# Values of memory heads 1 to 3 turned by VectorE and DMAs, and read nine steps later

## Chip, cores, metric

The kernel runs on one core of a Trainium2 chip. The time is the device time of one execution in microseconds (us); lower is better. The engines are TensorE (PE in the profile; PEld are its weight loads), VectorE (DVE), ScalarE (ACT), GpSimd (POOL) and SyncE (SP), whose queue issues nearly all DMAs here.

## What is computed

One inference step of a layer with two branches: a matrix memory (mLSTM, 4 heads of 512) and an HGRN2 branch (8 heads of 128), merged by sigmoid gates. There are 512 prompt frames and 32 sample frames, 544 columns in all, and the model's width is 1024. Of the reference, the part around the change:

```python
proj = xn @ w_in[l]
u, v_m, z_m, ... = jnp.split(proj, ...)           # v_m: the memory's values, 4 heads x 512
c = silu(causal_conv(u));  qm = c @ w_qm;  km = c @ w_km * M_HD ** -0.5     # per head
s = jnp.einsum('bhtd,bhsd->bhts', q, k) * dmat
num = w_inter[..., None] * jnp.einsum('bhed,bhtd->bhte', C, q) + jnp.einsum('bhts,bhse->bhte', s, v)
h = num / jnp.maximum(jnp.abs(den), jnp.exp(-m_t))[..., None]
C_new = decay[..., None, None] * C + jnp.einsum('bhs,bhse,bhsd->bhed', w_last, v, k)
hm = (head_layernorm(h) + m_skip[l] * c) * jax.nn.silu(z_m)
ya = hm @ w_brm[l]
```

Both products that use v sum over frames, so v is needed with frames on the partitions. The projection leaves it the other way, with channels on the partitions.

## The kernel before

Products are made in fp32r: each operand is split into a high part (ScalarE's copy) and a low part (VectorE's difference, L205 for weights), and three matmuls replace one (high x high, high x low, low x high). Memory heads go one after another; each has its keys (k), queries (q), scores (sc, L1054), then `mchain`, then the branch product `stage_br` (ya, L229), which adds to a sum kept in DRAM.

Between these pieces TensorE works through a list of input projections, the *pump*. A projection unit for the heads is a *pair* (class `Two`) of two channel tiles, made by a seven-product scheme in blocks a11, s2, a12, s3, s1, a22, s4; consecutive pairs overlap. A block is two *steps*, a step is six matmuls of 272 columns (line L575, tile d). For heads 1 and 2 the list is values v0/v1, v2/v3, gates z0/z1, z2/z3, and the next head's conv inputs u0/u1, u2/u3: 84 steps. For head 3 it is v, z and the first HGRN unit: 70 steps. By the order in which the blocks are sorted, v1, v0, v3, v2 are finished after steps 14, 18, 28 and 32, z1, z0, z3, z2 after 42, 46, 56 and 60, u1 and u0 after 70 and 74. `pump.when` holds these numbers, `pump.done` counts steps made.

`mchain` is a generator. A `yield n` in it lets TensorE do n more steps before what follows is put into its order; TensorE's order is thus written out by hand, and what is ready early has no influence on it. All other engines and SP's queue are ordered by the scheduler at build time, each queue then runs in order. After the last v (step 32), before the change:

- four blocks b of 128 frames, each after the gap that VTGAP gives: four transposes of v on TensorE into a PSUM buffer (tile vt, L1210; two such buffers rotate), ScalarE's high part vh (L1213), VectorE's low part vl (L1214);
- the sample's 32 frames: POOL makes three copies side by side (vsm, L963), four transposes (vts, L1222), the split into vs;
- four steps, then the old memory's split (c0p, c0h, c0l) where it isn't done yet and the numerators: matmuls nm (L1313, the sample's L1289), with the new sample memory Cs (L1241) between them. Cs takes one of the four PSUM buffers with tag "h", which the pairs use as well: two to a pair, the first from its first block on, the second from its a12;
- VectorE's normalisation; for heads 1 and 2 the weighed keys are read back from DRAM (kwl, L1155), and six and three steps later the prompt's new memory is made (C, L1112); eleven steps after that y is turned back in four groups a step apart (yt, L1366), with hm made from each (L1372 to L1374, L147) as input of `stage_br`. In head 3, whose new memory comes at the kernel's end, yt comes fourteen steps after the numerators or when its z is done. Then the pump runs out and `stage_br` starts.

In heads 1 and 2 the numerators start at step 41 and the first yt stands at step 61; in head 3 they start at 42.

The keys of heads 1 to 3 are already turned another way, by `turn` (L973 to 979): VectorE transposes each 32 by 32 block in place (L975), and four DMAs write the tile to DRAM so that blocks land transposed, in runs of 32 floats; a later DMA reads frames as rows.

## Time and profile before

| | |
|---|---|
| median of 3 runs | 1104.61 us (1103.64 to 1105.09) |
| profiled execution | 1106.07 us, span in the trace 1104.3 us |
| TensorE busy | 1089.9 us (99%) |
| VectorE busy | 920.8 us (83%) |
| ScalarE busy | 712.2 us (64%) |
| GpSimd busy | 173.0 us (16%) |
| DMA queue of SP | 40.0% of 16 engines' time, 137.10 MB |

Busy times are sums over the span of 1104.3 us. Matmuls overlap in TensorE's array and their ends are modelled, so intervals between starts tell more than durations. In rows of the timeline the columns are start, duration, engine, line, operation, and out<-in by the program's names; a bracket gives the engine's idle time before the row and what ended it.

### The profile page before, as it was taken

The numbers are of one execution on the slowest core, as the hardware profiler recorded it, in microseconds if no ns is written. First come the engines' busy times: TensorE is split into PE (matmuls) and PEld (weight loads), VectorE is DVE, ScalarE is ACT, GpSimd is POOL, SyncE is SP. The second block draws the span as 40 slices with busy tenths as digits, with TensorE's granted clock in tenths as the row PEclk, the third lists the DMA queues.
The fourth block names the chain that finished last, engine by engine and source line by source line (L and its number), as shares of the span: only waits on it lengthen the run. The fifth ranks groups of instructions, "written<-read, shape, count | busy, mean of one in ns | idle before, by whom it ended". The sixth has DMA issues, their size and how long they took to land.

```text
span 1104.3 us, 23737 instructions
## 1 busy us (share of the span) xinstructions
PE 1089.9 (99%) x8765; PEld 1077.4 (98%) x8765; DVE 920.8 (83%) x1989; ACT 712.2 (64%) x1571; POOL 173.0 (16%) x417
## 2 busy tenths in 40 slices
PE   9999999999999999999999999999999999999998
PEld 9999999999999999999999999999999999999998
DVE  6986999679798596986898688999999888789885
ACT  6686656755666455664566478887777767445762
POOL 2122024111010130101100123322332100000000
PEclk9999999999999999999999999999999999999999
DMA  6223225634365344464556222122221353343743
GB/s 224 78 96 107 83 86 174 146 100 127 105 206 160 81 147 144 126 225 92 157 159 218 95 78 84 56 80 80 85 75 62 111 178 116 116 124 116 260 146 121
DMA packets 104781, 138.67 MB, mean 126 GB/s; under 512 B 35765, under 2 KB 43573, under 8 KB 104665
## 3 DMA queue, kind: packets, MB, share of 16 engines
q1 hardware_dynamic: 104496, 137.10, 40.0%
q8 instruction: 69, 1.13, 0.4%
q14 instruction: 48, 0.39, 0.1%
q10 hardware_dynamic: 168, 0.06, 0.0%
HBM read 110.96 MB, written 26.16 MB: 124 GB/s over the span
## 4 chain that ended last, share of the span: by engine, by line
PE 59%; DVE 12%; ACT 7%; issue 2%; DMA 0%; POOL 0%; DVEq 0%; ACTq 0%; POOLq 0%
PE d L575 26%; PE ya L229 6%; PE pg L2099 4%; PE yb L229 4%; PE C L1112 3%; PE q L229 3%; DVE ws L533 2%; PE k L229 2%; PE sc L1054 2%; DVE hkq L1836 2%; PE nm L1313 2%; PE ple L229 1%; DVE at L1852 1%; DVE ws L508 1%; ACT shared L1947 1%
## 5 line engine op out<-in xcount | busy, mean ns | idle before, releaser
L592 ACT COPY t<-d 128x272 f32<-128x272 f32 x126 | 47.5, 377 | 20.8 <-PE d L575 20.7
L1770 ACT COPY kmos<-hkq 128x256 f32<-128x256 f32 x56 | 23.9, 427 | 38.0 <-DVE hkq L1836 34.7
L1836 DVE TENSOR_TENSOR hkq<-hkq,hq 128x288 f32<-128x288 f32 (+1 forms) x96 | 41.4, 438 | 1.5
L1815 PE MATMUL pl<-hkq,kmos 128*128 128x128 f32 x224 | 35.5, 279 | 3.3 <-DVE hkq L1653 1.9
L801 DVE SCALAR_TENSOR_TENSOR cv<-ub,vec,cv 128x547 f32<-128x547 f32 x48 | 37.1, 782 | 0.4
L1815 PEld LDWEIGHTS pl<-hkq,kmos 128*128 128x128 f32 x224 | 30.0, 188 | 4.9 <-ACT kmos L1770 1.5
L1112 PE MATMUL C<-vh,kwl 128*128 128x256 f32 x96 | 27.0, 281 | 0.0
L1112 PE MATMUL C<-vl,kwh 128*128 128x256 f32 x96 | 26.9, 280 | 0.0
L1112 PE MATMUL C<-vh,kwh 128*128 128x256 f32 x96 | 26.8, 279 | 0.0
L1392 DVE TENSOR_TENSOR y<-ya,y 128x272 f32<-128x272 f32 x48 | 18.8, 434 | 8.0 <-PE ya L229 7.8
L1852 DVE COPY_PREDICATED at<-lmask,pl 128x256 f32<-128x256 uint8 x56 | 25.0, 446 | 0.0
L1313 PE MATMUL nm<-vh,sh 128*128 128x256 f32 x80 | 22.8, 285 | 1.0 <-ACT Co L1124 0.6
L1324 ACT COPY y<-nm 128x516 f32<-128x516 f32 x16 | 9.4, 588 | 21.5 <-PE nm L1313 21.5
L1313 PE MATMUL nm<-vl,sh 128*128 128x256 f32 x80 | 22.6, 282 | 0.0
L963 POOL COPY vsm<-vt 128x96 f32<-128x96 f32 x16 | 12.8, 809 | 62.2 <-DVE vt L599 43.9
L1313 PE MATMUL nm<-vh,sl 128*128 128x256 f32 x80 | 22.5, 281 | 0.0
L1068 ACT CAST sh<-dm 128x512 fp32r<-128x512 f32 (+3 forms) x16 | 7.4, 459 | 22.8 <-DVE dm L1062 22.8
L1054 PE MATMUL sc<-q,kh 128*128 128x512 f32 (+3 forms) x80 | 18.6, 321 | 0.0
L1243 DVE SCALAR_TENSOR_TENSOR c<-c,wi,Cs 128x256 f32<-128x256 f32 (+1 forms) x32 | 14.9, 471 | 4.1 <-PE Cs L1241 4.0
L1112 PEld LDWEIGHTS C<-vh,kwh 128*128 128x128 f32 x96 | 18.1, 189 | 0.0
L1112 PEld LDWEIGHTS C<-vl,kwh 128*128 128x128 f32 x96 | 18.1, 188 | 0.0
L1112 PEld LDWEIGHTS C<-vh,kwl 128*128 128x128 f32 x96 | 18.0, 188 | 0.0
(5767 smaller groups left out, 5164.6 us busy)
## 6 DMA issues: line engine op xcount, KB each, us to landing
ya_d<-y SPq DMA_DIRECT2D x32, 272.0 KB, 3.1
y<-ya_d SPq DMA_DIRECT2D x24, 272.0 KB, 3.1
c<-in_C SPq DMA_DIRECT2D x16, 258.0 KB, 3.6
out_Cs<-c SPq DMA_DIRECT2D x16, 258.0 KB, 2.6
out_Cp<-Co SPq DMA_DIRECT2D x15, 258.0 KB, 2.5
k_d<-kf SPq DMA_DIRECT2D x48, 68.0 KB, 2.0
x<-in_xT SPq DMA_DIRECT2D x8, 272.5 KB, 4.6
ya<-ya_d SPq DMA_DIRECT2D x8, 272.0 KB, 4.7
```

The source lines that it names most:

```text
L229: PE.matmul(both[b][:m, :TH], part(w, off + k * step, m, x), xx[:, half(b)], start=(k == 0 and j == 0), stop=(k == n - 1 and j == 2),)
L575: PE.matmul(ps, ww[:, c], xx, start=(start and k == 0 and j == 0), stop=end, skip_group_check=not start,)
L592: S.copy(t, ps)
L801: last = V.scalar_tensor_tensor(cv[:, :547], ub[:, j : j + 547], vcol(V_CW + 4 * ft + j), cv[:, :547], ALU.mult, ALU.add)
L1054: PE.matmul(pn[:, 0, :n], ks[f][x][:, j * P : (j + 1) * P], qs[f][y][:, NS + j * P : T], start=(f == 0 and i == 0), stop=(f == KH - 1 and ...
L1112: PE.matmul(pn[g], kw[b][x][:, f * P : (f + 1) * P], vv[b][y][:, VS[g]], start=(b == 0 and j == 0), stop=(b == NB - 1 and j == 2),)
L1313: PE.matmul(pn[:, g, VP[g] : VP[g] + VN[g]], st[j][x][:, (i - j) * P : (i - j + 1) * P], vv[j][y][:, VS[g]], start=(j == 0 and q == 0), st ...
L1770: S.copy(km.rearrange("p (n j c) -> p n j c", j=2, c=c), view(kk, HB, ((2 * c, NA // (2 * c)), (c - HB, 2), (1, c))),)
L1815: PE.matmul(pn[:, b * P : (b + 1) * P].rearrange("p (n j c) -> p j n c", j=2, c=c), km[:, b * P : (b + 1) * P], view(qq, b * P, ((HB + c, ...
L1836: V.tensor_tensor(x, x, t, ALU.mult)
L1852: V.copy_predicated(blocks2(at[:, :NA]), twice(lmask[:, li, :P]), blocks2(pn[:, :NA]))
L2099: PE.matmul(ps, part(w, k * P, P, x), xx[:, c], start=(k == 0 and j == 0), stop=(k == KD - 1 and j == 2))
```

## The change

For heads 1 to 3 the four transposes per block of frames and those for the sample leave TensorE. When a value tile is projected, `turn` now transposes it on VectorE in blocks of 32 by 32 and writes it to DRAM with four DMAs (16 a head). Five steps after the last value (VREAD[0]) `mchain` issues seven reads: four blocks of 128 frames into the place of vl, and the sample's frames three times. Five steps later (VREAD[1]) the splits into vh and vl start, a step apart, from SBUF and not from PSUM; four steps after the sample's split the numerators follow as before. They start at step 50 in heads 1 to 3. The first yt moves from step 61 to 70 in heads 1 and 2; in head 3 the four groups stand at steps 64 to 67 of 70. Head 0 keeps its transposes.

```diff
--- before.py
+++ after.py
@@ -40,10 +40,10 @@
 STEPS = (5, 4, 3, 4, 4, 4, 4)
 START = 2
 PDGAP = 1
-VGAPS = (0, 0, 0, 0)
+VREAD = (5, 5)
 ZN = 3
 FIRSTK, KTGAP, KWGAP = (3, 2, 1, 1, 1), (6, 14), (6, 3, 11)
-VTGAP = ((2, 1, 1, 1, 1), (1, 1, 1, 1, 1), (1, 1, 1, 1, 1), (0, 2, 2, 1, 1))
+VTGAP = (2, 1, 1, 1, 1), (0, 1, 1, 1, 1), (0, 1, 1, 1, 1), (0, 1, 1, 1, 1)
 GAPS = (20, 20, 20, 14)
 APART = 10
 FDELAY = (2, 2, 5)
@@ -820,11 +820,13 @@
         t["cc"].append(c)
         t["cs"].append(split(c[:, :T], f"cs{ft}"))
 
+    vt_d = [dr.tile([T, HD], F32, name=f"vt_d{h}") for h in range(MH)]
+
     def fill(h):
 
 
         def value(f, t):
-            st8[h]["vt"][f] = t
+            turn(vt_d[h], f, t)
 
         def gate(f, t):
             act = S.activation(t[:, :T], t[:, :T], AF.Silu)
@@ -848,7 +850,6 @@
         st8[h]["z"] = [None] * KH
         todo = []
         if h:
-            st8[h]["vt"] = [None] * KH
             todo += [pair("v", f, 16 + h * KH + f, lambda f: plain(eslot(f"vt{h}{f}")), value) for f in (0, 2)]
             todo += [pair("z", f, 32 + h * KH + f, lambda f: plain(eslot(f"z{h}{f}")), gate) for f in (0, 2)]
         else:
@@ -1199,34 +1200,46 @@
             return ch, cl
 
 
+        vv, vraw = [], []
+
+        def pair_v(b):
+            vv.append([slot(f"v{n}{h}{b}", F32R)[:, VA : VA + VW] for n in "hl"])
+            for x, y in zip(vv[b], (one4, zero4)):
+                G.tensor_copy(x[:, HD:VW], y)
+
+        def parted_v(raw, hi, dst, at=slice(None)):
+            with tc.high_priority():
+                S.copy(hi, raw)
+                return V.tensor_tensor(dst, raw[at], hi[at].bitcast(F32), ALU.subtract)
+
         if h:
-            yield max(0, max(pump.when["v", f] for f in range(KH)) - pump.done + VGAPS[h])
-        vt = t["vt"]
-        vv = []
+            yield max(0, max(pump.when["v", f] for f in range(KH)) - pump.done + VREAD[0])
+            for b in range(NB):
+                pair_v(b)
+                vraw.append(vv[b][1][:, :HD].bitcast(F32))
+                nc.sync.dma_start(vraw[b], vt_d[h][NS + b * P : NS + (b + 1) * P, :])
+            vr = slot(f"vr{h}")[: 3 * NS, :HD]
+            for i in range(3):
+                nc.sync.dma_start(vr[i * NS : (i + 1) * NS], vt_d[h][:NS, :])
+            yield VREAD[1]
         for b in range(NB):
             yield VTGAP[h][b]
-            pt = paux(f"vt{h}{b}")
+            if h == 0:
+                pair_v(b)
+                vraw.append(paux(f"vt{h}{b}")[:, 0, :])
+                for f in range(KH):
+                    PE.transpose(vraw[b][:, f * P : (f + 1) * P], t["vt"][f][:, NS + b * P : NS + (b + 1) * P], ident)
+            parted_v(vraw[b], vv[b][0][:, :HD], vv[b][1][:, :HD])
+        yield VTGAP[h][NB]
+        if h == 0:
+            vr = paux(f"vts{h}")[: 3 * NS, 0, :]
+            vsm, _ = triple(t["vt"], "vsm", t["copied"])
             for f in range(KH):
-                PE.transpose(pt[:, 0, f * P : (f + 1) * P], vt[f][:, NS + b * P : NS + (b + 1) * P], ident)
-            vh, vl = (slot(f"v{n}{h}{b}", F32R)[:, VA : VA + VW] for n in "hl")
-            with tc.high_priority():
-                S.copy(vh[:, :HD], pt[:, 0, :])
-                V.tensor_tensor(vl[:, :HD], pt[:, 0, :], vh[:, :HD].bitcast(F32), ALU.subtract)
-            G.tensor_copy(vh[:, HD:VW], one4)
-            G.tensor_copy(vl[:, HD:VW], zero4)
-            vv.append((vh, vl))
-        yield VTGAP[h][NB]
-        pt = paux(f"vts{h}")
-        vsm, copied = triple(vt, "vsm", t["copied"])
-        for f in range(KH):
-            PE.transpose(pt[: 3 * NS, 0, f * P : (f + 1) * P], vsm[:, f], ident)
+                PE.transpose(vr[:, f * P : (f + 1) * P], vsm[:, f], ident)
         vs = small("vs", [3 * NS, VW], F32R, bufs=1)
-        with tc.high_priority():
-            S.copy(vs[:, :HD], pt[: 3 * NS, 0, :])
+        lo = slice(NS, 2 * NS)
+        low = parted_v(vr, vs[:, :HD], vs[lo, :HD], lo)
         G.tensor_copy(vs[:, HD:VW], vone)
-        lo = slice(NS, 2 * NS)
-        with tc.high_priority():
-            low = V.tensor_tensor(vs[lo, :HD], pt[lo, 0, :], vs[lo, :HD].bitcast(F32), ALU.subtract)
         if h == 0:
             with tc.issue_after(low.ins):
                 for k in THEN:
```

## The prediction

> **What bounds the kernel now.** I read the page first: the span and the busy shares.

> ```profile
> span 1104.3 us, 23737 instructions
> PE 1089.9 (99%) x8765; PEld 1077.4 (98%) x8765; DVE 920.8 (83%) x1989; ACT 712.2 (64%) x1571; POOL 173.0 (16%) x417
> ```

> TensorE is busy 99% of the span, VectorE is second with 83%. So work taken from TensorE is time gained, as long as nothing makes TensorE wait. The profiled execution took 1106.07 us around its span of 1104.3; the runs' median is 1104.61, 0.13% less. I work out a difference and take it from the median. About 0.2% (2.2 us) is what a measurement of this kernel can tell from no change.

> Next I read TensorE's order where values are turned: the tile's row (min/median/max ns), then head 1's rows of the timeline, then two of the chain of waits (start, us, what).

> ```profile
> L1210 PE MATMUL vt<-ident,vt x64: 270/272/330, 111.6 to 551.4; 128*128 128x128 f32 x64
> 252.93 0.60 PE L1210 MATMUL vt<-ident,vt 128*128 128x128 f32 x4
> 254.12 0.60 PE L1210 MATMUL vt<-ident,vt 128*128 128x128 f32 x4
> 255.31 0.60 PE L1210 MATMUL vt<-ident,vt 128*128 128x128 f32 x4
> 256.94 0.66 PE L1210 MATMUL vt<-ident,vt 128*128 128x128 f32 x4 [0.29 <-DVE vl L1214]
> 258.19 0.60 PE L1222 MATMUL vts<-ident,vsm 128*96 128x128 f32 x4
> ...
> 257.60 0.75 PE d L575 x6
> 258.35 0.43 PE vts L1222 x4
> ```

> Matmuls overlap, so starts count, not durations: from one group of four transposes to the next with a step between them (six matmuls, 0.75) are 254.12 - 252.93 = 1.19 us. A group thus costs 1.19 - 0.75 = 0.44; the group for the sample's values costs 0.43. The next row shows that groups also wait: 256.94 - 255.31 = 1.63, that is 0.44 lost, because two PSUM buffers rotate and VectorE had not read the older.

> **The change, part by part.**

> 1. *Transposes out of TensorE.* Heads 1 to 3 lose four groups L1210 and one L1222 each: 15 x 0.44 = 6.6 us. All of it lies on TensorE's path.

> 2. *Waits that go with them.* TensorE's waits over heads 1 to 3 (200 to 620 us):

> ```profile
> PE Cs L1241 <- DVE c L1243: 0.9, 2, 0.6
> PE vt L1210 <- DVE vl L1214: 0.7, 2, 0.4
> PE vt L1210 <- DVE vt L599: 0.6, 1, 0.6
> ```

> The vt rows name 1.3; starts give more (0.44 where the row says 0.29), so I take 1.6. The Cs row needs counting in steps. A projection pair holds two of the four "h" PSUM buffers, the second only from its a12 block on. Numerators start at step 41 in heads 1 and 2: the pair z0/z1 still holds both (its a22 is half done), z2/z3 one, one is left, and each new-memory matmul waits until VectorE read the one before it. At step 50 z0/z1 is done, z2/z3 holds two and u0/u1 has not begun: two are left, and as in head 3, where no such row stands, they alternate. With the small losses around them 1.5 us go; zero would go if the buffers were freed late. Gains: 6.6 + 1.6 + 1.5 = 9.7.

> 3. *What VectorE and the DMAs get.* The nearest rows are those of the keys, which take this way already: instructions (min/median/max ns), DMAs (KB, us to landing), windows (length, then busy us of PE, PEld, DVE, ACT, POOL, clock, DMA share, GB/s), timeline.

> ```profile
> L975 DVE STREAM_TRANSPOSE kf<-kf x12: 731/740/746, 203.3 to 503.7; 128x544 f32<-128x544 f32 x12
> L979 SPq DMA_DIRECT2D k_d<-kf x48: 303/504/1302, 204.1 to 506.0; - x48
> k_d<-kf SPq DMA_DIRECT2D x48, 68.0 KB, 2.0
> L1155 SPq DMA_DIRECT2D kwl<-k_d x8: 382/382/391, 271.8 to 419.9; - x8
> kwl<-k_d SPq DMA_DIRECT2D x8, 256.0 KB, 5.1
> L1214 DVE TENSOR_TENSOR vl<-vt,vh x16: 681/684/692, 113.3 to 552.4; 128x512 fp32r<-128x512 f32 x16
> 240.00:248.00 8.00, 8.00 (x67) 8.00 (x67) 7.13 (x13) 5.29 (x12) 0.66 (x1) 1.00 0.82 261
> 248.00:256.00 8.00, 8.00 (x69) 8.00 (x68) 7.86 (x15) 5.57 (x12) 4.78 (x9) 1.00 0.41 135
> 249.48 0.68 DVE L205 TENSOR_TENSOR wa1236l<-wi36r,wa1236h 128x512 fp32r<-128x512 f32 x1
> 252.44 0.28 PE L575 MATMUL d<-xh,wa1236l 128*128 128x272 f32 x1
> ```

> VectorE: 12 x 0.74 = 8.9 us more, 3.0 in each head between steps 14 and 32, where (windows) it is busy 7.13 and 7.86 of 8. The cover is the lead of the weights' low parts over TensorE: 252.44 - (249.48 + 0.68) = 2.3 us at the tightest in head 1. Two transposes fall into each of the two bursts, 1.5 us against 2.3. Bounds: 0 if the lead swallows all, 8.9 if none. Nearer to the lead's end: 1.0 us in all.

> ScalarE's and VectorE's splits stay, reading SBUF for PSUM: nothing. POOL loses 12 copies for the sample (L963) and waits for nobody here: nothing.

> SP's queue: per head 16 writes at 0.50 = 8 us, 7 reads at 0.4 = 3 us. Each pair of values puts 4 us of issuing ahead of weight loads behind it, within the same lead; the DMA engines (0.82, 0.41 busy) have room. Counted in the 1.0.

> 4. *The new way's length.* Last value at step 32, numerators at 50: 18 steps x 0.75 = 13.5 us, with no TensorE transposes between. Needed: evacuation and transpose about 1.5 (two operations of 0.74 at most), four writes issued 2.0, landing 2.0, four reads issued 1.6, landing 5.1: 12.2. The first split (ScalarE's vh and VectorE's vl, 0.68 each at most) ends at 13.6, just in time. The 5.1 is for four reads in flight together, so the first may land earlier; the sample's values follow behind them, and the first new-memory matmul that reads them comes two groups of numerators later. I take 0 lost; bounds 0 and 3 a head.

> [...]

> 5. *Nine steps later: what comes next.* Numerators, the Cs stores (4 x 258 KB), key reads, C matmuls and Cp stores of heads 1 and 2 move by nine steps (6.7 us), in head 3 by eight; on SP they pass weight loads for blocks that TensorE reaches only after the C matmuls; that VectorE idles there (288 to 296 us below) says that those are ahead: 0. The last part, turning y back (yt) and making hm for the branch matmuls (ya), is now close to its reader.

> ```profile
> 304.23 14.87 PE d L575 x120
> 319.10 23.69 PE ya L229 x192
> 299.70 0.44 PE yt L1366 x4
> 300.14 0.11 PE yt L1367
> 309.68 0.68 DVE L205 TENSOR_TENSOR wa1210l<-wi10r,wa1210h 128x512 fp32r<-128x512 f32 x1
> 310.88 0.71 DVE L147 TENSOR_TENSOR hm7l<-c,hm7h 128x544 fp32r<-128x544 f32 x1
> 317.32 0.69 DVE L205 TENSOR_TENSOR wbm100l<-wbm10r,wbm100h 128x512 fp32r<-128x512 f32 x1
> L1372 DVE SCALAR_TENSOR_TENSOR c<-yt,vec,c 128x512 f32<-128x512 f32 x4 | 3.0, 746 | 0.0
> L1374 DVE TENSOR_TENSOR c<-c,z 128x544 f32<-128x544 f32 x4 | 2.9, 725 | 0.0
> L801 DVE SCALAR_TENSOR_TENSOR cv<-ub,vec,cv 128x547 f32<-128x547 f32 x3 | 2.3, 782 | 0.0
> L1373 DVE SCALAR_TENSOR_TENSOR c<-yt,vec,c 128x32 f32<-128x32 f32 x4 | 1.0, 246 | 0.0
> 288.00:296.00 8.00, 8.00 (x69) 8.00 (x68) 2.58 (x7) 2.87 (x7) 1.07 (x6) 1.00 0.38 138
> 312.00:320.00 8.00, 8.00 (x67) 8.00 (x66) 8.00 (x16) 6.95 (x16) 3.73 (x5) 1.00 0.56 181
> 589.14 23.69 PE ya L229 x192
> 588.90 0.72 DVE L147 TENSOR_TENSOR hm15l<-c,hm15h 128x544 fp32r<-128x544 f32 x1
> ```

> Heads 1 and 2: 20 steps (14.87) lie between the last yt and ya, 11 (8.2) will. From the first yt (299.70) to the last low part of hm (310.88 + 0.71) are 11.9 us; ya will come 4 x 0.55 + 14 x 0.75 = 12.7 after the first yt, so hm itself is just in time. But VectorE is full there (8.00 of 8), the low part of wbm was ready only 319.10 - 318.01 = 1.1 ahead, and the next head's first convolution now falls into the same stretch. What makes room is the idle 5.4 us before it (2.58 of 8 busy), in which weights get ahead. Bounds: 0; and, if all of hm (3.0 + 2.9 + 1.0 + 4 x 0.71 = 9.7), the convolution (2.3) and four weight parts (2.7) stand in one row behind the first yt (0.55), 15.3 against 12.7: 2.6 late. I take 1.0 each: 2.0.

> Head 3: nine steps lay between, as the last yt groups waited for the last z (step 60). Now yt comes at steps 64 to 67 and three steps (2.2) remain. ya starts 4 x 0.55 + 6 x 0.75 = 6.7 after the first yt and reads the fourth hm's low part 3 x 0.75 + 0.25 = 2.5 later, at 9.2. In head 1 that took 11.9, with three weight operations between (one is shown, 0.68) that can be done beforehand here: 9.9 to 11.9. Stall 0.7 to 2.7; I take 1.7.

> Sum: -9.7 (1, 2) + 1.0 (3) + 0 (4) + 2.0 + 1.7 (5) = -5.0 us: 1104.61 - 5.0 = 1099.6 us, or 1101.1 for a profiled execution beside 1106.07.

> **The rivals.**

> A. *All hidden.* No new wait: -9.7, 1094.9 us. For it: VectorE's idle time before yt, the lead of 2.3 over its 1.5. Against: head 3's three steps.

> B. *VectorE takes the gain back.* Step 5 pays its upper ends (2.6 + 2.6 + 2.7 = 7.9) and 2 us of step 3's 8.9 surface: -9.7 + 9.9, 1104.8 us. For it: the full windows.

> C. *Values come late, and it is slower.* TensorE's order is fixed, so numerators that wait stop it. Place: the reads of vt_d on SP. Price: in head 1 SP stood behind one weight load as long as this:

> ```profile
> 252.60 9.97 SPq L172 DMA_DIRECT2D wi9r<-in_w_in  x2
> ```

> If such a wait goes ahead of the reads with half its length (5.0), the numerators lose 5 in each head: -5.0 + 15: 1114.6 us. It decides from (5.0 + 2.2)/3 = 2.4 us of lateness a head. Against it: the wait stood when SP had nothing else to issue.

> D. *Transposes cost more than their starts show.* The median of 272 ns would make the 60 transposes worth 16.3 us: -5.0 - 16.3 + 6.6 = -14.7, 1089.9 us. The starts contradict it (0.44 / 4 = 0.11 each). [...]

> **How the numbers follow.** Forecast (-2.5 to -7.5) 0.48, A 0.20, B 0.16, C 0.13, D 0.03. Faster 0.48 + 0.20 + 0.03 = 0.71, same 0.16, slower 0.13. The range reaches from A to just over B, which leaves C and D out: 1094.5 to 1107.0; the forecast's own is 1097.1 to 1102.1.

> **What would show it.** TensorE without L1210 and L1222 in heads 1 to 3 and without Cs waits; 12 transposes of 0.74 more on VectorE; the head's first nm row not waiting for a vl split (step 4); ya of head 3 waiting some 2 us for hm, ya of heads 1 and 2 for wbm or hm by about 1 (step 5); matmuls d between steps 14 and 50 hardly waiting for low parts (step 3). Wrong if nm waits for DMAs, or if d waits for weights through whole stretches, or if nothing waits at all.

## The result: slower by 3%, and the profile after

The changed kernel takes 1136.9 us (median of 4 runs, 1136.6 to 1138.2), the kernel before 1104.4 in the same comparison: a ratio of 1.0295, interval 1.0279 to 1.031. The forecast of 1099.6 us was wrong in sign; no rival came near either (the highest, C, gave 1114.6).

The head of the page after:

```profile
span 1135.2 us, 23727 instructions
PE 1098.4 (97%) x8705; PEld 1083.4 (95%) x8705; DVE 931.6 (82%) x2001; ACT 711.6 (63%) x1571; POOL 154.4 (14%) x405
```

TensorE has 60 matmuls fewer, as planned, yet it is *busier* (1098.4 against 1089.9 us) in a span 30.9 us longer. Two things must have happened: it stands idle, and its matmuls last longer. The first is told by TensorE's waits (us in total, times, longest):

```profile
PE nm L1326 <- ACT vh L1212: 7.6, 3, 2.5
PE Cs L1254 <- DVE vs L1213: 6.8, 3, 2.3
PE nm L1326 <- DVE vl L1213: 3.6, 3, 1.2
PE d L575 <- DVE vt L601: 3.2, 3, 1.1
PE ya L229 <- ACT hm14h L146: 2.9, 1, 2.9
...
PE ya L229 <- ACT hm15h L146: 1.0, 1, 1.0
```

Four waits come three times, once in each of heads 1 to 3: for the first block's vh and vl, for the sample's values vs, and, a little earlier, for a values tile (vt) that VectorE puts together late. Together they are 7.1 us a head. Two more are in head 3 alone, at its branch product.

The second is told by the windows (length, busy us and instructions of PE, PEld, DVE, ACT, POOL, then the granted clock, DMA share, GB/s). Before, the numerators of head 1:

```profile
262.60:272.80 10.20, 9.90 (x74) 8.81 (x74) 8.71 (x23) 3.78 (x7) 0.00 (x0) 1.00 0.45 150
```

After, the numerators of head 1 and the branch product of head 3:

```profile
270.30:280.50 10.20, 7.65 (x34) 7.35 (x35) 8.52 (x17) 4.52 (x9) 0.53 (x1) 0.50 0.14 52
618.50:625.30 6.80, 6.00 (x25) 5.75 (x26) 3.44 (x6) 3.25 (x6) 0.24 (x1) 0.50 0.40 139
```

The granted clock is 0.50 there. In the timeline, just behind two idle times, the numerators' matmul takes 0.42, where its group on the page of before has a mean of 0.285:

```profile
269.02 0.38 PE L1326 MATMUL nm<-vh,sh 128*128 128x256 f32 x1 [2.55 <-ACT vh L1212]
270.60 0.58 PE L1326 MATMUL nm<-vl,sh 128*128 128x256 f32 x1 [1.20 <-DVE vl L1213]
...
271.84 0.42 PE L1326 MATMUL nm<-vh,sh 128*128 128x256 f32 x1
...
275.59 0.58 PE L1254 MATMUL Cs<-vs,kws 96*128 96x256 f32 x1 [2.25 <-DVE vs L1213]
...
577.08 0.38 PE L1326 MATMUL nm<-vh,sh 128*128 128x256 f32 x1 [2.55 <-ACT vh L1212]
```

The last row is the first numerators' matmul of head 3; its wait is that of head 1 to the digit.

Why are vh, vl and vs late? First SP's queue, from the put of the last values tile on (a row is start, us of issuing):

```profile
253.74 1.51 SPq L172 DMA_DIRECT2D wi38r<-in_w_in  x1
255.34 2.10 SPq L980 DMA_DIRECT2D vt_d<-vt  x4
257.49 1.97 SPq L172 DMA_DIRECT2D wi8r<-in_w_in  x1
259.56 1.79 SPq L172 DMA_DIRECT2D wi9r<-in_w_in  x2
261.53 1.75 SPq L1220 DMA_DIRECT2D vl<-vt_d  x4
```

The writes wait behind one weight load, the reads behind three: 4.1 us lie between the last write and the first read, of which the writes' own landing takes 2.1 (the median of the 48 writes). The reads of head 1's blocks land 3.9 to 4.5 us after issue, the first of them at 261.53 + 3.9 = 265.4. TensorE comes to the numerators at 269.02 - 2.55 = 266.47. In head 3 the first read, issued at 569.60, took 3.0 us and was there at 572.6, TensorE came at 574.53. So the first block's rows were there 1.1 and 1.9 us ahead, and the wait is 2.55 us in both heads: it isn't set by the rows' landing. Then ScalarE's order:

```profile
266.51 0.39 ACT L592 COPY t<-d 128x272 f32<-128x272 f32 x1 [1.40 <-PE d L575]
266.79 0.62 ACT L204 CAST wa118h<-wi8r 128x512 fp32r<-128x512 f32 x1
...
267.83 0.62 ACT L204 CAST wa2238h<-wi39r 128x512 fp32r<-128x512 f32 x1
268.35 0.62 ACT L1212 CAST vh<-vl 128x512 fp32r<-128x512 f32 x1
...
272.08 0.59 ACT L1337 COPY y<-nm 128x516 f32<-128x516 f32 x1
...
273.09 0.62 ACT L1212 CAST vs<-vr 96x512 fp32r<-96x512 f32 x1
```

The first vh runs at 268.35, behind a copy of the last projection result (t), which itself waits for TensorE until 266.51, and behind three weight parts that TensorE multiplies only after the numerators. The sample's vs runs behind the copy of the *first numerators' result* (y), so it can't run until TensorE has done these, whenever its data came. With VectorE's low part of vs 1.8 us later, Cs waits. Each queue runs in the order that was fixed at build time. Why the scheduler put the splits at these places isn't known.

### The profile page after: what moved, and what is told of

Its sections match the earlier page's. It is cut to its first block, busy times and chain, and to the rows that moved or that the text cites. A ratio compares the mean times of both kernels' runs of the same rounds, so it can differ in the third digit from the quotient of the medians.

```text
span 1135.2 us, 23727 instructions
## 1 busy us (share of the span) xinstructions
PE 1098.4 (97%) x8705; PEld 1083.4 (95%) x8705; DVE 931.6 (82%) x2001; ACT 711.6 (63%) x1571; POOL 154.4 (14%) x405
## 4 chain that ended last, share of the span: by engine, by line
PE 71%; DVE 15%; ACT 9%; issue 3%; DMA 1%; SPq 1%; POOL 0%; ACTq 0%; DVEq 0%; POOLq 0%
PE d L575 26%; PE ya L229 8%; PE k L229 4%; PE pg L2112 4%; PE yb L229 4%; PE q L229 4%; PE C L1113 4%; DVE ws L533 2%; PE u L355 2%; PE sc L1055 2%; PE v L229 2%; PE nm L1326 2%; DVE hkq L1849 2%; PE d L455 1%; PE ple L229 1%
## 5 line engine op out<-in xcount | busy, mean ns | idle before, releaser
L801 DVE SCALAR_TENSOR_TENSOR cv<-ub,vec,cv 128x547 f32<-128x547 f32 x48 | 37.1, 782 | 0.5
L1326 PE MATMUL nm<-vh,sh 128*128 128x256 f32 x80 | 26.7, 334 | 8.2 <-ACT vh L1212 7.6
L1326 PE MATMUL nm<-vl,sh 128*128 128x256 f32 x80 | 27.0, 337 | 3.6 <-DVE vl L1213 3.6
L1326 PEld LDWEIGHTS nm<-vh,sh 128*128 128x128 f32 x80 | 19.1, 239 | 9.3 <-ACT vh L1212 8.3
L1326 PE MATMUL nm<-vh,sl 128*128 128x256 f32 x80 | 26.3, 329 | 0.0
L1326 PEld LDWEIGHTS nm<-vl,sh 128*128 128x128 f32 x80 | 19.2, 240 | 4.2 <-DVE vl L1213 4.2
L1256 DVE SCALAR_TENSOR_TENSOR c<-c,wi,Cs 128x256 f32<-128x256 f32 (+1 forms) x32 | 15.1, 475 | 5.7 <-PE Cs L1254 5.7
L1326 PEld LDWEIGHTS nm<-vh,sl 128*128 128x128 f32 x80 | 19.2, 240 | 0.0
L321 POOL COPY ub<-vec 128x3 f32<-128x3 f32 x16 | 4.8, 300 | 103.7 <-DMA vt_d<-vt 44.9
## 6 DMA issues: line engine op xcount, KB each, us to landing
vl<-vt_d SPq DMA_DIRECT2D x12, 256.0 KB, 4.4
```

The source lines that it names most:

```text
L801: last = V.scalar_tensor_tensor(cv[:, :547], ub[:, j : j + 547], vcol(V_CW + 4 * ft + j), cv[:, :547], ALU.mult, ALU.add)
L1326: PE.matmul(pn[:, g, VP[g] : VP[g] + VN[g]], st[j][x][:, (i - j) * P : (i - j + 1) * P], vv[j][y][:, VS[g]], start=(j == 0 and q == 0), st ...
```

## Experiments

My theory was: (A) lateness and the queues' order make TensorE idle, idle time halves its clock, and head 3 has a loss of its own. Rivals: VectorE's extra work is the loss (B); the nine steps themselves are (C).

**Nine steps without the new way.** The kernel before with TensorE's transposes, numerators nine (head 3: eight) steps later:

```diff
-        yield 4
+        yield 4 + (0, 9, 9, 8)[h]
```

> The kernel before, with the values still turned by TensorE at the same steps, but nine more steps (eight in head 3) between the sample's values and the numerators: the delay alone. Theory A: Cs waits go (-1.5), head 3's branch product waits as in the changed kernel (+5 and some 3 for the clock): about 1111 us. Theory C: 1130 or more. Theory B: 1104, nothing but the head 3 part.

Measured 1111.8 us, ratio 1.0064 (1.0049 to 1.0079). Its waits at ya, hm14h 2.9 and hm15h 1.0 us, are those of the changed kernel to the digit, and the halved clock comes behind them too:

```profile
593.50:600.30 6.80, 5.99 (x25) 5.73 (x26) 3.44 (x6) 3.27 (x6) 0.24 (x1) 0.50 0.41 139
```

The delay in heads 1 and 2 alone was tried later, as (0, 9, 9, 0):

> The kernel before with the numerators of heads 1 and 2 alone nine steps later (TensorE still turns the values; head 3 untouched). Theory A (the delay by itself takes the Cs waits of about 0.5 us a head away in heads 1 and 2 and costs nothing there; in head 3 it cost the 6.8 us of halved clock and 3.9 us of ya waits): 1104.0 - 1 to 2 = about 1102.5 (1101.5 to 1104). Rival (the delay costs in every head alike, 7.8 / 3 us each): about 1109.

Measured 1103.5 us, ratio 0.9989 (0.998 to 0.9998), 1.3 us less than its 1104.7. So the delay costs 7.8 + 1.3 = 9.1 us in head 3 and nothing in heads 1 and 2, and C, which expected 1130 or more, is out. It is the one version here that comes out below the kernel before, by 0.02 to 0.2%, which is hardly more than can be told.

**VectorE's and SP's work without the way.** The kernel before, with the values transposed by VectorE into tiles of their own and written to DRAM, all unread:

```diff
+            turn(vt_d[h], f, t, slot(f"tt{h}{f}"))
             st8[h]["vt"][f] = t
```

> The kernel before, plus VectorE's 12 transposes of the values of heads 1 to 3 (into tiles of their own) and the 48 writes to DRAM, which nobody reads; TensorE still turns the values it uses. The cost of that load alone. Theory A: d waits of some 1.2 + 0.3 us a head, 4 us in all, no drop of the clock: about 1108 us. Theory B: 1125 or more.

Measured 1110.6 us, ratio 1.0056 (1.004 to 1.0073), far from B's 1125 or more. One wait is new:

```profile
PE d L575 <- DVE vt L601: 4.4, 3, 1.7
```

VectorE's order shows its place: before (first two rows), and with the extra work (the last three).

```profile
248.53 0.43 DVE L601 SCALAR_TENSOR_TENSOR vt<-d,t 128x272 f32<-128x272 f32 x1
...
249.48 0.68 DVE L205 TENSOR_TENSOR wa1236l<-wi36r,wa1236h 128x512 fp32r<-128x512 f32 x1
```

```profile
248.43 0.69 DVE L205 TENSOR_TENSOR wa1236l<-wi36r,wa1236h 128x512 fp32r<-128x512 f32 x1
249.26 0.69 DVE L205 TENSOR_TENSOR ws336l<-ws,ws336h 128x512 fp32r<-128x512 f32 x1
249.87 0.43 DVE L601 SCALAR_TENSOR_TENSOR vt<-d,t 128x272 f32<-128x272 f32 x1
```

The put of vt, for which TensorE's next block needs the PSUM buffer, stood ahead of two low parts and now stands behind them. Is it the load or the order? The same kernel without the writes (`turn` ends after the transpose):

> The kernel before with the twelve transposes of the values by VectorE alone (into tiles of their own that nobody reads; no writes to DRAM). VectorE's order is then that of the kernel before at the place that made d wait: the put of the fourth values tile (L601) stands ahead of the low parts ws422l and wa1236l, where with the writes it stands behind them. Theory A (a step's order, not VectorE's load, makes the d waits of 1.2 to 1.9 us a head): d doesn't wait for vt, and the time is 1105 (1103.5 to 1106.5). Rival (VectorE's 0.74 us a transpose are the loss, wherever the put stands): d waits for vt again, about 1110.

Measured 1106.5 us beside 1103.6: ratio 1.0024 (1.0015 to 1.0034), at the upper end of what A expected. No row of d for vt is left; VectorE, still with the twelve transposes, puts vt earlier again:

```profile
248.63 0.43 DVE L601 SCALAR_TENSOR_TENSOR vt<-d,t 128x272 f32<-128x272 f32 x1
...
250.18 0.75 DVE L205 TENSOR_TENSOR wa1236l<-wi36r,wa1236h 128x512 fp32r<-128x512 f32 x1
```

So of the 6.6 us the transposes are 2.9; the rest comes with the writes, and with it the other order on VectorE. That the order alone makes it, and not the writes' traffic, is seen for the waits of d (4.4 us) and is not shown for the remainder.

**Idle time filled.** The changed kernel with 20 matmuls of 512 columns ahead of the first numerators of heads 1 to 3 and 12 ahead of the first Cs, results unused:

```diff
+            if h and i == 0:
+                pz = paux(f"fill{h}a")
+                for _ in range(20):
+                    PE.matmul(pz[:, 0, :], st[0][0][:, :P], st[0][0], start=True, stop=True)
...
+                if h and i == 1 and j == 0:
+                    pz = paux(f"fill{h}b")
+                    for _ in range(12):
```

> The changed kernel with matmuls of 512 columns whose result nobody reads, 20 ahead of the first numerators of heads 1 to 3 and 12 ahead of the first new-memory matmul: TensorE is busy (about 7.5 us a head) where it idled (6.7). If the idle time is what halves the clock for 10.2 us in each head, that goes and 3 to 3.5 us a head are gained in spite of the added work: about 1127 us and a clock of 1.0 in heads 1 to 3 (head 3's branch product still drops). If the clock falls for another cause, 1137 or a little more. Theories B and C say nothing of the clock: 1137.

Measured 1131.4 us, 5.4 *less* than the changed kernel's 1136.9 with 96 matmuls more (ratio to before 1.0241, 1.0226 to 1.0256); 9 or 10 less were expected. Its timeline, and the window 275.7 to 280.5 us, first of the changed kernel and then of this one:

```profile
266.47 4.71 PE L1325 MATMUL fill1a<-sh 128*128 128x512 f32 x20
...
272.82 3.02 PE L1340 MATMUL fill1b<-sh 128*128 128x512 f32 x12 [0.21 <-ACT y L1345]
275.76 0.38 PE L1254 MATMUL Cs<-vs,kws 96*128 96x256 f32 x1
```

```profile
275.70:280.50 4.80, 4.80 (x23) 4.80 (x24) 3.19 (x7) 0.59 (x1) 0.47 (x1) 0.50 0.15 55
```

```profile
275.70:280.50 4.80, 4.80 (x37) 4.45 (x37) 4.77 (x13) 1.18 (x2) 0.53 (x1) 1.00 0.16 58
```

The first Cs starts at nearly the same moment (275.76, without the fill 275.59): the fill took the idle time and little more. What follows runs at 1.00 and makes 37 matmuls in the time of 23. The 23 would thus have taken 4.8 x 23 / 37 = 3.0 us, 1.8 less a head, and the times say 5.4 / 3 = 1.8 too. The granted clock is 1.00 from 266.0 to 276.2 us as well, and 0.996 over the whole execution, where the changed kernel has 0.983. That idle time halved the clock in these heads is shown; the halved clock ahead of 275.7 costs nothing more, since Cs would have waited anyway, and that is why less came back than the 3 to 3.5 us a head expected.

**Rows that are there in time.** The changed kernel with its seven reads taking the rows of k, in DRAM long before:

```diff
-                nc.sync.dma_start(vraw[b], vt_d[h][NS + b * P : NS + (b + 1) * P, :])
+                nc.sync.dma_start(vraw[b], k_d[h][NS + b * P : NS + (b + 1) * P, :])
```

> The changed kernel, but the seven reads per head fetch the keys' rows, which lie in DRAM long before, in place of the turned values; turning on VectorE, the 48 writes, the reads, the splits and all steps stay. So nothing waits for the values' way through DRAM any more (what is computed with them is not the reference). Theory A (values come late, TensorE idles before the numerators and its clock is halved after it): the waits of nm and Cs (18 us over three heads) and about 10 us of half clock go; what is left is -9.7 for the transposes, some 4 us of d waits in steps 14 to 50 and 8 us at head 3's branch product: 1104.4 - 9.7 + 4.4 + 8.4 = 1107.5 us. Theory B (VectorE's transposes, the writes and reads load the engines and queues): stays near 1137. Theory C (nine steps later is the cost): stays near 1137.

Measured 1136.3 us (ratio 1.0286, 1.027 to 1.0301): nothing gained, a clear miss for a theory of lateness alone. (What this kernel computes with k's rows isn't the reference's result.) The time is what B and C expected here, but of the 32 us the kernels above give 7.8 to the delay and 6.6 to VectorE's work, so neither explains it.

```profile
PE Cs L1254 <- DVE vs L1213: 13.5, 3, 4.7
PE d L575 <- DVE vt L601: 6.6, 3, 2.3
```

The numerators wait no longer, but Cs waits twice as long (13.5 against 6.8), and so does d for vt. The sample's rows were issued by 261.4 and landed 2.7 us later, but ScalarE (rows of this kernel) got to them nine us after:

```profile
259.41 1.96 SPq L1223 DMA_DIRECT2D vr<-k_d  x3
```

```profile
271.52 0.59 ACT L1337 COPY y<-nm 128x516 f32<-128x516 f32 x1
...
273.04 0.62 ACT L1212 CAST vs<-vr 96x512 fp32r<-96x512 f32 x1
```

Queue order by itself is enough for the Cs wait. Two further tries at lateness and order:

> The changed kernel with the numerators of heads 1 to 3 another four steps later (some 3 us of projection work more between the reads of the turned values and their use; in head 3 the transposes that follow keep their step). Theory A (two separate causes: the values land 2.7 + 1.5 us late, and the sample's split stands behind the copy of the first numerators in ScalarE's queue whatever the lateness): the numerators' waits of 3.7 us a head go with a part of the halved clock (1.8 us a head), the Cs wait of 2.3 us a head stays: 1136.3 - 3 x 5.5 = about 1120. Rival (lateness of the way through DRAM is all): the Cs wait goes too, 1136.3 - 3 x (6.7 + 3.5) = about 1106. Rival (neither; VectorE's extra work is what costs): no change, about 1136.

(`VREAD = (5, 9)`, `GAPS = (20, 20, 20, 10)`.) Measured 1139.6 us (1.0319, 1.0305 to 1.0333), none of the expected times. The nearest is the 1136 of the rival in which VectorE's extra work is what costs, and the unread work above, 6.6 us in all, rules that out. The numerators' waits went, as A said, but Cs then waited 10.7 us for vs, 2.4 for c, and yt 3.6. Giving time does not help what stands behind y in the queue; it moves the stall.

> The changed kernel with the sample's rows read and split ahead of the four blocks in heads 1 to 3; the numerators keep their step. In ScalarE's queue all five splits now stand ahead of the copy of the first numerators, but behind the three weight parts wa118h, ws138h and wa2238h, and the reads land no sooner. Theory A (two causes): the Cs wait of 2.3 us a head goes, the wait at the first numerators grows by the sample's split and its place behind the last read (1 to 3 us a head), one long stall in place of three; the sum moves little: 1133 (1129 to 1137). Rival (queue order alone, data in time): no more than 1.5 us of stall a head and about 1117.

(`vr` read and split ahead of the loop over the blocks.) Measured 1136.2 us (1.0288, 1.0274 to 1.0302). The Cs wait (6.8) is gone, and the numerators wait 19.3 where they waited 11.2:

```profile
PE nm L1333 <- ACT vh L1212: 12.3, 3, 4.1
PE nm L1333 <- DVE vl L1213: 7.0, 3, 2.4
```

**Head 3 apart.** Head 3 alone on TensorE's transposes at its old step (`turn` for `h < MH - 1` only, `VTGAP[3] = (0, 2, 2, 1, 1)`):

> The changed kernel with head 3 alone put back: TensorE turns its values, its numerators come at the old step. Heads 1 and 2 stay on the way through DRAM. Theory A (head 3 lost 9.2 us to its ya and 8.7 us from its ya to the next stage, all of it by its own waits and halved clock, and nothing of that comes back elsewhere): 1136.3 - 17.9 = about 1118.5 (1117 to 1121), heads 1 and 2 keep + 7.2 us each. Rival (each head costs the same, a third of the 32 us): about 1126. Rival (TensorE isn't what sets the end there, another stall takes the place): 1130 or more.

Measured 1122.8 us, ratio 1.0163 (1.0149 to 1.0176), 14.1 less, outside A's range and about halfway between A (17.9) and equal shares (10.8). What is left is 1122.8 - 1104.7 = 18.0, that is 9.0 each if all of it is heads 1 and 2; but 1.4 of it is a wait in head 3 (the sample's transposes vts for a low part vl), which the kernel before doesn't have. So head 3 loses at least 5.1 more than each of the others. Where is seen on ScalarE in the changed kernel (hm14h and hm15h go into the waiting ya):

```profile
612.28 1.28 ACT L1655 ACT_TABLE_LOAD   x1
613.58 0.66 ACT L1655 ACTIVATE hkq<-tf 128x544 f32<-128x544 f32 x1
...
616.11 0.63 ACT L146 CAST hm14h<-c 128x544 fp32r<-128x544 f32 x1
616.76 1.28 ACT L1656 ACT_TABLE_LOAD   x1
...
618.61 0.63 ACT L146 CAST hm15h<-c 128x544 fp32r<-128x544 f32 x1
```

VectorE's last operation on hm14's data ended at 614.07, so about 2.0 of the 2.9 us at ya are the place in the queue (616.11). Before, both splits ran ahead of the first of these loads (586.61 and 587.78, the load 589.25). With `GAPS[3]` 8 in place of 14, yt comes sooner and they do so again:

> The changed kernel with one number changed: in head 3 the transposes of the normalised numerators come 8 steps after them in place of 14. In ScalarE's queue hm14h and hm15h then stand ahead of the HGRN activations with their three table loads (1.28 us each), as they did in the kernel before. Theory A (the ya waits of 4.6 us and the 6.8 us at half clock behind them come from that order): both go, 1136.5 - 4.6 - 3.4 = about 1128.5 (1127 to 1130). Rival (the halved clock and the stall move to the transposes, which now come too soon after the normalisation): 1133 or more. Heads 1 and 2 unchanged.

Measured 1131.9 us (1.0254, 1.0238 to 1.027), 5.0 less than the changed kernel: between A (8 less) and its rival. No wait of ya for hm14h or hm15h is left there, and the granted clock over the whole execution is 0.986 beside the changed kernel's 0.983, as it would be without the 6.8 us at half (0.5 x 6.8 / 1135.2 = 0.003), but yt now waits 1.6 us for VectorE's normalised y. So the order on ScalarE was the cause of most of it, and part of the gain is paid back.

**Both removed.** Two kernels with head 3 as before. In the first, heads 1 and 2 read the rows of k, the sample's first:

> Heads 1 and 2 as in the changed kernel, but their reads fetch the rows of k (in DRAM long before, so the output is not the reference's) in place of the turned values, and the sample's rows are read and split ahead of the four blocks; head 3 put back to TensorE's transposes at its old step. The turning by VectorE and its writes stay. Theory A (lateness plus queue order make the waits and the halved clock; VectorE's extra work costs about 2 us a head): no wait at numerators and Cs, so 1104 - 2 x 3.45 (transposes and old waits saved) + 2 x 2.2 = about 1101.5 (1099 to 1105). Rival (VectorE's extra work and the splits brought forward cost what was saved): 1108 to 1112 with d waiting for vt. Rival (the Cs wait is not of queue order): Cs still waits 4 us a head with the halved clock, about 1113.

Measured 1116.8 us (1.0106, 1.0091 to 1.0122), above A's 1101.5 and both rivals. The Cs wait is gone, but nm waits 4.5 us for vh. ScalarE's rows:

```profile
269.55 0.59 ACT L1350 COPY y<-nm 128x516 f32<-128x516 f32 x1 [0.32 <-PE nm L1339]
...
271.60 1.66 ACT L1216 CAST vh<-vl 128x512 fp32r<-128x512 f32 x3
```

Blocks 1 to 3 were there at about 267 (issued to 263.0, 4.6 to landing) but stood behind y and three weight parts. The second kernel uses the real values, six steps later than the change (`VREAD = (5, 11)`, `KWGAP = (4, 3, 6)`), the sample first; all five splits then stand ahead of y:

> Heads 1 and 2 on the way through DRAM with six steps more between the reads and the numerators (fifteen later than in the kernel before; the gaps of what follows are shortened so that it still ends in the head), the sample's rows read and split first, so that all five splits stand ahead of the copy of the first numerators in ScalarE's and VectorE's queues; head 3 as in the kernel before. Theory A (lateness and queue order cause the stalls; VectorE's extra work costs 1.5 to 2.2 us a head by itself): no stall at numerators and Cs and no halved clock in heads 1 and 2: 1104.7 - 2 x 3.45 + 2 x 2 = about 1102 (1099.5 to 1105). Rival (the splits are late at any distance, because each moves with its place in the queues): nm or Cs waits of 2 us or more a head and 1112 or more.

Measured 1112.5 us, ratio 1.008 (1.0066 to 1.0094). The numerators and vs are waited for no more, as A said, but the time is 10 us above what A made of it, and is the rival's (1112 or more), though not by its waits of numerators or Cs:

```profile
PE d L575 <- DVE vt L601: 2.1, 2, 1.1
...
PE d L575 <- ACT wa118h L204: 1.5, 1, 1.5
PE d L575 <- ACT wa1112h L204: 1.5, 1, 1.5
```

With the numerators gone from their place, TensorE comes to the next projection block sooner and waits for that block's weight part, the very wa118h that had stood ahead of vh. The stall has changed its name once more. By the starts of the projection matmuls (as in the table below) head 1 takes 3.3 us more than in the kernel before, head 2 2.8 and head 3 1.4. In heads 1 and 2 the waits of d come to 2.9 and 3.0 us, in head 1 with 3.4 us of halved clock behind them; in head 3 it is the wait of 1.4 at vts again. The rows thus name the larger part; why the order came out so is not known, and no kernel here keeps the gain of taking the transposes off TensorE.

## Why the prediction was wrong, by its steps

1. *Transposes out of TensorE, -6.6*: the work is gone as said (60 matmuls fewer). It was gained and then given back elsewhere.
2. *Waits that go, -3.1*: right. No wait for c at Cs and none at vt is left in heads 1 to 3. The delay alone in heads 1 and 2 gave 1.3 us of the 1.5. In the changed kernel nothing came of that part, as Cs waits for vs there.
3. *VectorE and SP, +1.0*: mis-sized, 6.6 measured (unread work), inside its bounds of 0 to 8.9, but not near the 1.0 taken. I asked whether the transposes fit into the lead of the weights' low parts. That was the wrong question: the put of vt changed places with two low parts, and TensorE waits for it 1.1 us a head in the changed kernel.
4. *The way's length, 0*: the step that failed first. The length itself was nearly right: from the end of step 32 (252.55) to the landing of the first block (265.4) are 12.9 us, with the two splits (0.62 and 0.69) 14.2, and TensorE came 13.9 us after that step: 0.3 late by the data alone. I added up the ways of the data (12.2 of 13.5 us) and left out what stands ahead in the queues, on ScalarE above all: a copy that waits for TensorE and three weight parts ahead of vh, and y ahead of vs. Lost: 2.5 + 1.2 + 2.3 = 6.0 us a head where I had 0 with bounds of 0 and 3. The prediction's rival C also had it slower by numerators that wait, and they did wait more than its 2.4 us a head (3.7). But its place was SP's queue and its cause lateness. SP did stand behind weight loads with reads to issue, against C's own objection, some 2 us more than the writes' median landing asked for; the first rows still came in time, and with rows that were there long before, the loss stayed.
5. *Nine steps later*: for heads 1 and 2 I took 1.0 each, and no ya wait came. For head 3 I took 1.7 (0.7 to 2.7), from VectorE's operations; the rows say 2.9 + 1.0. I had looked at one of the two engines that make hm: ScalarE's copies hm14h and hm15h ended up behind activations of the HGRN branch with table loads.

*And one thing was in no step: the clock.* Every new wait was priced by its own length. With waits of 1 to 3 us in a row, the granted clock went to 0.50 for 10.2 us in each of the three heads (from 270.3, 423.9 and 577.5 on) and for 6.8 in head 3's ya (from 618.5 on). What could be had back behind the waits is 1.8 us a head, by the filled kernel.

How it adds up can be read from both traces, since the projection matmuls (d) come in the same order in both. The table has the start of the first of them in each head's list, and of the first behind head 3's ya (us):

| | head 1 | head 2 | head 3 | behind ya | end |
|---|---|---|---|---|---|
| before | 220.07 | 366.31 | 512.94 | 612.67 | 1104.3 |
| after | 219.19 | 373.25 | 527.16 | 643.79 | 1135.2 |

Head 1 thus takes 7.8 us more, head 2 7.3 and head 3 16.9, 32.0 together; the parts ahead and behind take 0.9 and 0.2 less, which gives the span's 30.9. In head 1 the waits are 7.1, and the numerators' matmuls take 2.8 more by their starts, idle times left out (9.97 and 12.75 us); against that stand the five groups (2.2) and the waits of before at vt and Cs (0.6): 7.1 of the 7.8. In head 3 the waits are 7.1 + 3.9 at ya, the numerators take 3.2 more (9.28 and 12.47) and ya 3.7 (23.70 and 27.44), less 2.2 + 0.6: 15.1 of the 16.9. What is left, 1.8 in head 3 and under 1 in head 1, I leave open. The slow numerators ahead of Cs are in these sums; without them Cs would have waited longer instead.

## What to carry to other kernels

Where engines run in queues whose order is fixed at build time, ask of each new instruction not only when its data is there, but what stands ahead of it in its queue, and whether that itself waits for the engine that you want to feed; print the order of every queue that the change touches, and compare it with the one before. Here 6.6 us of work were taken off the busiest engine, and the new path for the same data crossed three queues (SP, ScalarE, VectorE) that were full of other work. Read the granted clock behind each new wait on TensorE as well: behind 2.55 and 1.20 us in the changed kernel the granted clock was 0.50 for 10.2 us, behind 2.9 and 1.0 at head 3's ya for 6.8. With the unread work, where d waited 1.7 us at the longest, the clock was 1.0 over the whole execution.

## What the hardware showed that I had not expected

```profile
269.40:272.80 3.40, 3.40 (x18) 3.40 (x17) 3.30 (x6) 2.40 (x6) 0.53 (x1) 0.50 0.30 81
419.00:422.40 3.40, 3.40 (x30) 3.40 (x28) 3.30 (x6) 2.41 (x6) 0.51 (x1) 1.00 0.30 77
```

- A table load took ScalarE 1.28 us in the rows of head 3's branch product, and no step of the prediction has one. The activation starts at 613.58, 0.02 us behind the end of the first (612.28 + 1.28).
